# A decoder trunk in fp32 on one core: v's 512-column chunk goes first, and the first norm's gain moves behind the transposes

## The chip, the cores and the metric

The kernel runs on one core of one Trainium2 chip. The metric is the device time of one execution in microseconds (us). For the kernel before it is 1230.37, the median of three runs (1230.25 to 1230.64). One further execution was taken with the hardware profiler, and all rows of the trace come from it.

The engines are named as in the profile: PE (TensorE matmul), PEld (its weight loads), DVE (VectorE), ACT (ScalarE), POOL (GpSimd), SP (SyncE, which only issues DMAs here). L312 is line 312 of the kernel.

## The reference, cut to what matters

x has 512 tokens of 1024 features; there are two layers. The first mixes with a forgetting attention, the second with a gated short convolution; each is followed by a squared-ReLU MLP and a gated embedding. The change touches only the first norm and the first projections of the attention:

```python
def rmsnorm(x, g):
    y = x * lax.rsqrt(jnp.mean(x * x, axis=-1, keepdims=True) + RMS_EPS)
    return y * g

hn = rmsnorm(x, g[0])
proj = hn @ w_attn_in              # q, k, v: 1024 columns each; 16 forget-gate logits
v, f_logit = proj[..., 2*D:3*D], proj[..., 3*D:] + b_f
c = cumsum(log_sigmoid(f_logit))   # enters the scores as c_i - c_j
```

## The kernel before

**Numbers.** Everything is fp32. A factor is split in two fp32r parts, hi and lo (`split`, L270: ACT copies hi, then DVE or POOL subtracts it from the source for lo), and a product is three matmuls: hi*hi, lo*hi and hi*lo (`mm3`, L262).

**Layout.** The 512 tokens are four blocks of 128; a block's 1024 features are two pages of 128 x 512. `hT` holds the normed tokens turned, features on partitions, as a hi and a lo tile of eight 128-feature slices. A turned half block fills one bank of PSUM with four 128x128 transposes (`turned`, L309), and `keep` (L315) splits the whole bank into `hT`: one 128x512 copy on ACT, one 128x512 subtraction on DVE.

**The first norm.** `stats` (L298) squares both halves of a block on ACT (L295) with their sums, and `rstd` (L284) adds them and raises to the power -0.5 on POOL (L287, L290). `scaled` (L301) multiplies x by the inverse root and by the gain in one DVE operation (L303). The gain must stand in all 128 partitions: two 2 KB rows are loaded by POOL's DMAs and spread by PE's matmuls on a row of ones (L970 to L983) into two PSUM banks, which L303 reads.

**v.** `values(c, t)` (L438) makes one chunk c of v's columns for block t: eight features' slices, three matmuls each. `V_CHUNKS` gives the chunks and their order: first the last 256 columns of v together with the 16 logits (272 columns), then 512, then 256 columns. The function that it returns, `keep_v`, adds b_f to the logits (L454) and splits v into the pages `vs` by 128x128 copies and subtractions. So 96 matmuls stand behind each chunk: 4 blocks x 8 slices x 3.

**Weights.** `plan` lists all weights in order of use; `fetch` (L151) loads them on SP into 14 raw buffers, and `prepare` (L174) splits them into pages wh and wl, some eight ahead of use.

**What orders the work.** Within `manual_schedule` the order of the named engines is the one in the program's text; elsewhere a scheduler sets it. The opening is by hand on PE, DVE and ACT (L619 to L633): the norm of block 0, the first weights, then the four blocks through the 272-column chunk, each block's transposes in the middle (ahead of slice 5) of the block before. The loads of x and of the first eight weights are by hand on SP and ACT (L975 to L980), with b_f's load ahead of them on SP by the scheduler.

**After the opening.** `logs` (L397) makes log sigmoids of all logits, `sums_of_logs` (L419) their running sums by eight matmuls on a triangle (`tri`, L643) into `ps_c`; the sums go to DRAM and come back spread over partitions by `bias` (L498), with a select on POOL (L511). Then `project` (L470) makes q and k of two heads at a time (tile qk, 512 columns), and the scores (L516) begin. The first qk matmul is the first matmul behind v.

## Time and profile before

| | |
|---|---|
| median of three runs | 1230.37 us |
| the profiled execution | 1230.79 us |
| its span in the trace | 1229.1 us |
| mean granted PE clock | 0.997 |
| ACT busy | 676.4 us (55%) |
| POOL busy | 657.1 us (53%) |
| DMA, mean over the span | 121 GB/s |

The span runs from the first to the last instruction that the trace shows; a time in a row is counted from its start. A timeline row gives the start, the time from there to the end of the last of its instructions, the engine, line and operation, output<-inputs, shapes and count, and in brackets the idle time of the engine before it with what ended it. Matmuls are pipelined: the time of one in a row is longer than the distance of two starts. A row of a group gives after the count the busy time and the mean of one in ns, then the engine's idle time before them. A row of PE's waits gives us in total, times, and the longest. A row of windows gives the length, then the busy time of PE, PEld, DVE, ACT and POOL with their instructions, the granted PE clock, the share of the DMA engines and GB/s.

### The profile page before, as it was taken

The page shows a single profiled execution, that of the slowest core. Times are in us where ns is not written, and L with a number is a line of the kernel's source. Part 1 is how long each engine was busy: PE and PEld are TensorE (multiplying, and loading weights), DVE is VectorE, ACT ScalarE, POOL GpSimd, SP SyncE. Part 2 cuts the span into 40 slices and gives each one's busy share as a digit, 9 for nine tenths or more (in the row PEclk, how much of TensorE's full clock was granted, in tenths as well). Part 3 has the DMA queues.
Part 4 walks back from the last instruction along what each step waited for, and adds up shares of the span by engine and source line. Part 5 has one row for each costly group of instructions (what it writes and reads, how often), then busy time and mean ns, then how long its engine had stood idle before and what let it go on. Part 6 is the DMA issues. An engine that isn't in the chain of part 4 may idle for free.

```text
span 1229.1 us, 18662 instructions
## 1 busy us (share of the span) xinstructions
PE 1210.3 (98%) x6188; PEld 1030.5 (84%) x6188; DVE 912.2 (74%) x1410; ACT 676.4 (55%) x1429; POOL 657.1 (53%) x619
## 2 busy tenths in 40 slices
PE   7999999999999999999999999999999999999997
PEld 6888888898888888888889999989888888888886
DVE  5648878676778767869877798867776787669873
ACT  5447777556744654455565544445756345645551
POOL 2016656244977787775213255316677878678210
PEclk9999999999999999999999999999999999999999
DMA  7456564542343324428133033552422443236401
GB/s 251 149 157 172 143 172 113 167 149 78 103 137 105 98 73 137 132 68 296 57 100 108 30 104 95 156 174 74 137 78 60 137 138 99 64 113 180 162 18 52
DMA packets 85793, 148.73 MB, mean 121 GB/s; under 512 B 10112, under 2 KB 17328, under 8 KB 85696
## 3 DMA queue, kind: packets, MB, share of 16 engines
q1 hardware_dynamic: 85488, 147.27, 39.2%
q8 instruction: 49, 0.80, 0.3%
q14 instruction: 48, 0.39, 0.1%
q10 hardware_dynamic: 144, 0.26, 0.1%
q0 software_dynamic: 64, 0.00, 0.0%
HBM read 136.93 MB, written 6.37 MB: 117 GB/s over the span
## 4 chain that ended last, share of the span: by engine, by line
PE 96%; ACT 1%; DVE 1%; DMA 1%; issue 1%; POOL 1%; SPq 0%; DVEq 0%; POOLq 0%; ACTq 0%
PE up L266 9%; PE up L265 9%; PE up L264 9%; PE dn L264 8%; PE dn L265 8%; PE dn L266 8%; PE qk L265 2%; PE qk L264 2%; PE qk L266 2%; PE pg L265 2%; PE pg L264 2%; PE pg L266 2%; PE n_p L312 1%; PE pT L539 1%; PE v L264 1%; PE v L265 1%
## 5 line engine op out<-in xcount | busy, mean ns | idle before, releaser
L273 DVE TENSOR_TENSOR wl<-raw,wh 128x512 fp32r<-128x512 f32 (+1 forms) x398 | 377.3, 991 | 22.3 <-ACT wh L272 21.3
L272 ACT CAST wh<-raw 128x512 fp32r<-128x512 f32 (+1 forms) x398 | 217.5, 620 | 4.6 <-DVE xd L348 4.4
L265 PE MATMUL up<-hTh,wl 128*128 128x512 f32 (+1 forms) x576 | 210.2, 365 | 0.0
L266 PE MATMUL up<-hTl,wh 128*128 128x512 f32 (+1 forms) x576 | 209.7, 366 | 0.0
L264 PE MATMUL up<-hTh,wh 128*128 128x512 f32 (+1 forms) x576 | 208.7, 366 | 0.0
L820 ACT ACTIVATE r<-up 128x512 f32<-128x512 f32 (+1 forms) x72 | 39.4, 547 | 203.2 <-PE up L266 201.0
L273 POOL TENSOR_TENSOR wl<-dn_T,wh 128x512 fp32r<-128x512 f32 x96 | 132.6, 1413 | 30.1 <-ACT wh L272 30.1
L167 POOL TENSOR_TENSOR dn_T<-raw,raw 128x512 f32<-128x512 f32 x56 | 86.9, 1563 | 68.8 <-DMA raw<-in_wdn 58.3
L265 PEld LDWEIGHTS up<-hTh,wl 128*128 128x128 f32 x576 | 108.6, 189 | 17.5
L264 PEld LDWEIGHTS up<-hTh,wh 128*128 128x128 f32 x576 | 108.6, 189 | 17.6
L266 PEld LDWEIGHTS up<-hTl,wh 128*128 128x128 f32 x576 | 108.3, 189 | 17.5
L866 DVE TENSOR_TENSOR acc<-dn,acc 128x512 f32<-128x512 f32 x168 | 107.3, 679 | 14.9 <-PE dn L266 14.8
L167 POOL TENSOR_TENSOR dn_T<-raw,dn_T 128x512 f32<-128x512 f32 x56 | 92.4, 1650 | 2.2
L272 ACT CAST wh<-dn_T 128x512 fp32r<-128x512 f32 x112 | 61.4, 616 | 11.1 <-POOL dn_T L167 11.1
L273 DVE TENSOR_TENSOR A12l<-q,A12h 128x512 fp32r<-128x512 f32 x28 | 22.4, 801 | 55.0 <-ACT A12h L272 54.9
L880 POOL TENSOR_TENSOR acc<-acc,acc 128x512 f32<-128x512 f32 x28 | 46.9, 1706 | 9.9 <-DVE acc L866 9.9
L265 PE MATMUL qk<-hTh,wl 128*128 128x512 f32 x128 | 51.0, 399 | 0.0
L266 PE MATMUL qk<-hTl,wh 128*128 128x512 f32 x128 | 51.0, 398 | 0.0
L264 PE MATMUL qk<-hTh,wh 128*128 128x512 f32 x128 | 50.9, 398 | 0.0
L265 PE MATMUL pg<-wh,hTl 128*128 128x512 f32 x128 | 50.5, 394 | 0.0
L264 PE MATMUL pg<-wh,hTh 128*128 128x512 f32 x128 | 50.4, 394 | 0.0
L273 DVE TENSOR_TENSOR A11l<-q,A11h 128x256 fp32r<-128x256 f32 x28 | 23.1, 825 | 36.5 <-ACT A11h L272 36.5
(371 smaller groups left out, 3244.4 us busy)
## 6 DMA issues: line engine op xcount, KB each, us to landing
raw<-in_wup SPq DMA_DIRECT2D x128, 256.0 KB, 2.9
raw<-in_wdn SPq DMA_DIRECT2D x128, 256.0 KB, 2.8
raw<-in_wcq SPq DMA_DIRECT2D x36, 256.0 KB, 2.8
raw<-in_wqk SPq DMA_DIRECT2D x32, 256.0 KB, 3.4
raw<-in_wpg SPq DMA_DIRECT2D x32, 256.0 KB, 4.3
g<-in_g SPq DMA_DIRECT2D x22, 256.0 KB, 5.3
prl<-neg_c SPq DMA_DIRECT2D x16, 256.0 KB, 6.7
raw<-in_wo SPq DMA_DIRECT2D x16, 256.0 KB, 5.9
```

Source lines behind the costliest of these rows:

```text
L167: ins = nc.gpsimd.tensor_tensor(out=B[name], in0=B[a], in1=B[b], op=op)
L264: nc.tensor.matmul(ps, a.hi, b.hi, start=start, stop=False)
L265: nc.tensor.matmul(ps, a.lo, b.hi, start=False, stop=False)
L266: nc.tensor.matmul(ps, a.hi, b.lo, start=False, stop=stop)
L272: nc.scalar.copy(hi, src)
L273: return eng.tensor_tensor(out=lo, in0=src, in1=hi.bitcast(F32), op=ALU.subtract)
L312: nc.tensor.transpose(ps[:, j * P : (j + 1) * P], h[:, j * P : (j + 1) * P], ident)
L539: nc.tensor.transpose(ps[:, b * P : (b + 1) * P], probs[h][b][:, j * P : (j + 1) * P], ident)
L820: nc.scalar.activation(r[:, :n], ps[:, :n], AF.Relu)
L866: ins = nc.vector.tensor_tensor(out=a, in0=banks[s], in1=a, op=ALU.add)
L880: nc.gpsimd.tensor_tensor(out=a, in0=a, in1=acc[i, s][:, :S], op=ALU.add)
```

## The change

Five things change, all in the opening.

- **Order of the chunks.** The 512-column chunk comes first, then 272, then 256. The logits thus come with the second chunk: `logs` stands behind it, `sums_of_logs` behind block 2 of the third.
- **Two blocks through half the weights at a time.** The order is written out by hand on PE, DVE, ACT and now POOL: block 0 through weights 0 to 3, block 1 through them, block 0 through 4 to 7, then block 1; then blocks 2 and 3 as `values` does them. A block's hi*hi and lo*hi products of several slices go ahead of their hi*lo products. The lo parts of weights 0, 1, 2, 4, 5 and 6 are subtracted on POOL, those of 3 and 7 on DVE, each at a place of its own. The transposes of block 2 stand behind block 0's last product, those of block 3 behind block 1's.
- **The norm.** One half is squared on ACT, the other on DVE with its sum; DVE adds, POOL takes the power; DVE scales x by the inverse root without the gain.
- **The gain** is loaded as a column per slice (`g_col`, 128 x 8, on SP behind the first half block of x). `keep_rows` takes the place of `keep`: for each 128x128 piece of a bank ACT copies it times the gain to hT's hi, and DVE multiplies again and subtracts hi for lo. The gain's rows, PE's matmuls on ones that spread them, and their banks go.
- **Matmuls on ones.** `work(12)` issues twelve 128x512 matmuls on a page of ones, into a bank that nothing reads, ahead of the first transposes.

b_f is loaded behind x. The scheduler still orders the rest.

```diff
@@ -29,7 +30,7 @@
 PAGES = 70
 RAWS = 14
 LEAD = 1
-V_CHUNKS = ((768, 272), (0, 512), (512, 256))
+V_CHUNKS = ((0, 512), (768, 272), (512, 256))
 SOON = 8
 O_SOON = 1
 FEW = 4
@@ -66,7 +67,7 @@
 
 
 @with_exitstack
-def trunk(ctx: ExitStack, tc, x, pT, g, wv, wqk, bf, wo, wci, wcq, cw, wco, wup, wdn, wpp, wpg, out):
+def trunk(ctx: ExitStack, tc, x, pT, g, gT, wv, wqk, bf, wo, wci, wcq, cw, wco, wup, wdn, wpp, wpg, out):
     nc = tc.nc
     pool = lambda name, bufs, **k: ctx.enter_context(tc.tile_pool(name=name, bufs=bufs, **k))
     consts = pool("consts", 1)
@@ -171,7 +172,11 @@
                     mybir.DependencyInfo(mybir.DependencyClass.Sync, mybir.DependencyReason.DATA),
                 )
 
-    def prepare(upto):
+    def low_part(lo, src, hi, eng):
+        return eng.tensor_tensor(out=lo, in0=src, in1=hi.bitcast(F32), op=ALU.subtract)
+
+    def prepare(upto, held=None):
+
         while begun[0] < min(upto, len(order)):
             n = begun[0]
             begun[0] += 1
@@ -187,7 +192,11 @@
                 fetch(at + 1)
                 raw, eng, w = fetched[at], nc.vector, loads[at].shape[-1]
                 fetched[at] = None
-            split(hi[:, :w], lo[:, :w], raw[:, :w], eng)
+            if held is None:
+                split(hi[:, :w], lo[:, :w], raw[:, :w], eng)
+            else:
+                nc.scalar.copy(hi[:, :w], raw[:, :w])
+                held.append(partial(low_part, lo[:, :w], raw[:, :w], hi[:, :w]))
             ready[key] = Pair(hi[:, :w], lo[:, :w])
 
     def wide(*key, soon=SOON):
@@ -295,6 +304,14 @@
         nc.scalar.activation(junk, src, AF.Square, scale=D**-0.5, accum_out=ss)
         return ss
 
+    def products(src, name):
+        ss = stat(name)
+        nc.vector.tensor_tensor_reduce(
+            out=page(f"{name}_sq")[:, :S], in0=src, in1=src, scale=1.0 / D, scalar=EPS,
+            op0=ALU.mult, op1=ALU.add, accum_out=ss,
+        )
+        return ss
+
     def stats(t, xs, name):
         return rstd([squares(xs[n][:, :S], f"{name}_q{n}_{t}") for n in range(2)], f"{name}_r{t}")
 
@@ -385,9 +402,7 @@
                          f"{kind}r")
                 then(t)
 
-    def attention(hT, first_x, g0, by_hand):
-        b_f = consts.tile([P, H], F32, tag="bf", name="b_f")
-
+    def attention(hT, first_x, g_col, by_hand):
         vs = [[page(f"v{t}_{i}", F32R) for i in range(4)] for t in range(NB)]
         n_f = NB * H
         logit = stat("logit", n_f)
@@ -435,18 +450,17 @@
                 )
                 nc.sync.dma_start(neg_c[b, :, :n], t[:H, :n])
 
-        def values(c, t, soon=SOON, between=None):
+        def values(c, t, ps=None):
 
             c0, width = V_CHUNKS[c]
             n_v = min(width, D - c0)
-            ps = bank(f"v{c}_{t}")
-            for k in range(KT):
+            done = ps is not None
+            ps = ps if done else bank(f"v{c}_{t}")
+            for k in () if done else range(KT):
                 if width == 256:
                     w = wide("v", c, k // 2).at(lambda u: u[:, k % 2 * 256 : k % 2 * 256 + 256])
                 else:
-                    w = wide("v", c, k, soon=soon)
-                if k == 5 and between:
-                    between()
+                    w = wide("v", c, k)
                 mm3(ps[:, :width], tokens(hT, k, t), w, k == 0, k == KT - 1)
 
             def keep_v():
@@ -601,38 +615,111 @@
             prepare(where["o", 1, KT - 1] + 1)
             yield from out_part((0, 1), (6,))
 
-        nc.sync.dma_start(b_f, bf[0:1, :].partition_broadcast(P))
-        name = "n0"
-        E, done_v = mybir.EngineType, []
-
-        def rows(t):
-            r = stats(t, first_x[t], name)
-            return [scaled(t, n, first_x[t], r, g0, name) for n in range(2)]
+        name, E = "n0", mybir.EngineType
+        turns, banks_v = {}, [bank(f"v0_{t}") for t in range(2)]
+
+        def mean_squares(t):
+            half = lambda n: first_x[t][n][:, :S]
+            return squares(half(0), f"{name}_q0_{t}"), products(half(1), f"{name}_q1_{t}")
+
+        def inverse(t, q):
+            v, r = stat(f"{name}_v{t}"), stat(f"{name}_r{t}")
+            nc.vector.tensor_tensor(out=v, in0=q[0], in1=q[1], op=ALU.add)
+            nc.gpsimd.tensor_tensor(out=r, in0=v, in1=neg_half, op=ALU.pow)
+            return r
+
+        def scale_rows(t, r):
+            hs = []
+            for n in range(2):
+                hs.append(page(f"{name}_h{t}_{n}"))
+                nc.vector.tensor_scalar(
+                    out=hs[n][:, :S], in0=first_x[t][n][:, :S], scalar1=r, scalar2=None,
+                    op0=ALU.mult,
+                )
+            return hs
 
         def turn_rows(t, hs):
             for n in range(2):
-                keep(t, n, turned(t, n, hs[n], name), hT)
-
-        with tc.manual_schedule(engines={E.PE, E.DVE, E.Activation}):
-            r = stats(0, first_x[0], name)
-            prepare(3)
-            hs = {0: [scaled(0, n, first_x[0], r, g0, name) for n in range(2)]}
-            prepare(4)
+                turns[t, n] = turned(t, n, hs[n], name)
+
+        def keep_rows(t, n):
+            ps = turns.pop((t, n))
+            for j in range(4):
+                k = 4 * n + j
+                src, h = ps[:, j * P : (j + 1) * P], tokens(hT, k, t)
+                nc.scalar.mul(h.hi, src, g_col[:, k : k + 1])
+                nc.vector.scalar_tensor_tensor(
+                    out=h.lo, in0=src, scalar=g_col[:, k : k + 1], in1=h.hi.bitcast(F32),
+                    op0=ALU.mult, op1=ALU.subtract,
+                )
+
+        def part(t, k, p, of, start=False, stop=False):
+            nc.tensor.matmul(
+                banks_v[t], getattr(tokens(hT, k, t), p), getattr(ready["v", 0, k], of),
+                start=start, stop=stop,
+            )
+
+        def parts(t, ks, order, stop=False):
+            for p, of in order:
+                for k in ks:
+                    part(t, k, p, of, k == 0 and p == of, stop and k == ks[-1] and of == "lo")
+
+        HH, LH, HL = ("hi", "hi"), ("lo", "hi"), ("hi", "lo")
+        held = []
+
+        def low(eng):
+            held.pop(0)(eng)
+
+        with tc.manual_schedule(engines={E.PE, E.DVE, E.Activation, E.Pool}):
+            work(12)
+            r = inverse(0, mean_squares(0))
+            hs = scale_rows(0, r)
+            prepare(3, held)
+            low(nc.gpsimd)
+            low(nc.gpsimd)
+            turn_rows(0, hs)
+            keep_rows(0, 0)
+            prepare(4, held)
+            r = inverse(1, mean_squares(1))
+            parts(0, range(3), (HH, LH))
+            parts(0, range(3, 4), (HH, LH))
+            parts(0, range(2), (HL,))
+            last = held.pop()
+            last(nc.vector)
+            hs = scale_rows(1, r)
+            low(nc.gpsimd)
+            turn_rows(1, hs)
+            keep_rows(1, 0)
+            keep_rows(0, 1)
+            prepare(KT, held)
+            parts(1, range(4), (HH, LH))
+            parts(0, range(2, 4), (HL,))
+            parts(1, range(4), (HL,))
+            low(nc.gpsimd)
+            low(nc.gpsimd)
+            r = inverse(2, mean_squares(2))
+            hs = scale_rows(2, r)
+            low(nc.gpsimd)
+            keep_rows(1, 1)
+            low(nc.vector)
+            parts(0, range(4, KT), (HH, LH, HL), True)
+            turn_rows(2, hs)
+            r = inverse(3, mean_squares(3))
+            hs = scale_rows(3, r)
             for n in range(2):
-                keep(0, n, turned(0, n, hs[0][n], name), hT)
-                prepare(5 + n)
-            prepare(KT)
-            hs[1] = rows(1)
-            hs[2] = rows(2)
-            for t in range(NB):
-                between = (lambda: turn_rows(t + 1, hs[t + 1])) if t + 1 < NB else None
-                done_v.append(values(0, t, 0, between))
-                if t + 3 < NB:
-                    hs[t + 3] = rows(t + 3)
-                if t:
-                    prepare(KT + 3 * t)
-                    done_v.pop(0)()
-        done_v.pop(0)()
+                keep_rows(2, n)
+            values(0, 0, banks_v[0])()
+            parts(1, range(4, KT), (HH, LH, HL), True)
+            turn_rows(3, hs)
+            for n in range(2):
+                keep_rows(3, n)
+            values(0, 1, banks_v[1])()
+            for t in (2, 3):
+                done = values(0, t)
+                prepare(KT + 4 * t - 4, held)
+                while held:
+                    low(nc.gpsimd if len(held) % 2 else nc.vector)
+                done()
         tri = page("tri", F32R)
         ones = page("ones")
         nc.gpsimd.memset(ones[:, :S], 1.0)
@@ -641,15 +728,15 @@
             pattern=[[1, S]], channel_multiplier=-1,
         )
         nc.vector.tensor_copy(tri[:, :S], ones[:, :S])
+        for t in range(NB):
+            values(1, t)()
         logs()
         for t in range(NB):
-            values(1, t)()
+            values(2, t)()
             if t == 2:
                 sums_of_logs(tri)
         bias(0)
         bias(1)
-        for t in range(NB):
-            values(2, t)()
         for _ in project(0):
             pass
         main = stream()
@@ -967,24 +1054,28 @@
                 then(t)
 
 
-    one = page("one")
-    nc.vector.memset(one[:1, :P], 1.0)
-    rows = [page(f"row{n}") for n in range(2)]
-    for n in range(2):
-        nc.gpsimd.dma_start(rows[n][:1, :], g[0:1, n * S : (n + 1) * S])
+    warm = page("warm", F32R)
+    nc.vector.memset(warm[:, :S].bitcast(F32), 1.0)
+    g_col = consts.tile([P, KT], F32, tag="g_col", name="g_col")
     with tc.manual_schedule(engines={mybir.EngineType.SP, mybir.EngineType.Activation}):
         first_x = [load_x("xa", 0)]
+        nc.sync.dma_start(g_col, gT)
         fetch(4)
         first_x.append(load_x("xc", 1))
         fetch(KT)
         first_x += [load_x("xc", t) for t in (2, 3)]
-    g0 = [bank(f"g0_{n}") for n in range(2)]
-    for n in range(2):
-        nc.tensor.matmul(g0[n], one[:1, :P], rows[n][:1, :], start=True, stop=True)
+        b_f = consts.tile([P, H], F32, tag="bf", name="b_f")
+        nc.sync.dma_start(b_f, bf[0:1, :].partition_broadcast(P))
+
+    def work(n):
+        ps = bank("warm_p")
+        for _ in range(n):
+            nc.tensor.matmul(ps, warm[:, :P], warm[:, :S], start=True, stop=True)
+
     kept = dram.tile([2, NB, 2, P, S], F32, tag="kept", name="kept")
     hT = turned_x
     by_hand = ExitStack()
-    lhs, opened = attention(hT, first_x, g0, by_hand)
+    lhs, opened = attention(hT, first_x, g_col, by_hand)
     oT = lhs
     lhs = lambda k, t: tokens(oT, k, t)
     kind = "o"
@@ -1060,6 +1151,7 @@
 
     wa = np.asarray(w_attn_in)[0]
     got = {"x": np.asarray(x)[0], "g": np.asarray(norm_g).reshape(12, D)}
+    got["gT"] = got["g"][0].reshape(KT, P).T
     got["pT"] = np.asarray(p)[:, 0].reshape(2, S, 2, P).transpose(0, 3, 2, 1)
     for c, (c0, w) in enumerate(V_CHUNKS):
         got[f"wv{c}"] = tiles(wa[:, 2 * D + c0 : 2 * D + c0 + w], 2 if w == 256 else 1, w)[0]
```

1 line of the change is left out of this document (added).

## The prediction

> **What bounds the kernel now.** First the page: span, busy shares, the slices, the chain that ended last.
>
> ```profile
> span 1229.1 us, 18662 instructions
> ...
> PE 1210.3 (98%) x6188; PEld 1030.5 (84%) x6188; DVE 912.2 (74%) x1410; ACT 676.4 (55%) x1429; POOL 657.1 (53%) x619
> ...
> PE   7999999999999999999999999999999999999997
> ...
> PE 96%; ACT 1%; DVE 1%; DMA 1%; issue 1%; POOL 1%; SPq 0%; DVEq 0%; POOLq 0%; ACTq 0%
> ```
>
> PE is busy 98% of the span, in every slice but the first and the last, and 96% of the chain is PE. So the change, which touches only the opening, can move the end only by the time at which PE gets through that opening. I read PE's waits next, then PE's timeline.
>
> ```profile
> PE g L983 <- DMA row<-in_g: 6.4, 1, 6.4
> PE n_p L312 <- DVE n_h L303: 1.8, 1, 1.8
> 10.04 2.03 PE L312 MATMUL n_p<-ident,n_h 128*128 128x128 f32 x8
> 16.91 1.84 PE L312 MATMUL n_p<-ident,n_h 128*128 128x128 f32 x8 [1.84 <-DVE n_h L303]
> 19.00 0.43 PE L266 MATMUL v<-wl,hTh 128*128 128x272 f32 x1
> 19.23 0.43 PE L264 MATMUL v<-wh,hTh 128*128 128x272 f32 x1
> 21.06 0.29 PE L265 MATMUL v<-wh,hTl 128*128 128x272 f32 x1
> 21.19 0.29 PE L266 MATMUL v<-wl,hTh 128*128 128x272 f32 x1
> 22.44 1.03 PE L312 MATMUL n_p<-ident,n_h 128*128 128x128 f32 x8
> 23.23 0.37 PE L264 MATMUL v<-wh,hTh 128*128 128x272 f32 x1
> 36.22 0.39 PE L264 MATMUL v<-wh,hTh 128*128 128x512 f32 x1
> 36.45 0.39 PE L265 MATMUL v<-wh,hTl 128*128 128x512 f32 x1
> 47.78 0.40 PE L423 MATMUL ps_c<-tri,lf_h 128*16 128x512 f32 x1
> 48.95 0.44 PE L264 MATMUL v<-wh,hTh 128*128 128x512 f32 x1
> 54.48 0.28 PE L264 MATMUL v<-wh,hTh 128*128 128x256 f32 x1
> 65.99 0.40 PE L264 MATMUL qk<-hTh,wh 128*128 128x512 f32 x1
> ```
>
> The first column is the start. PE stands 6.4 us until the gain's rows land, spreads the gain, turns block 0 at 10.04, stands 1.8 us for block 1, and issues the first qk matmul at **65.99**. Start to start at full clock, a transpose takes 0.10 ((23.23 - 22.44)/8), a v matmul 0.125 at 272 columns, 0.227 at 512 ((47.78 - 36.22)/51, the count of such starts), and 0.12 at 256 ((65.99 - 54.48)/96); the sums of logs take 1.17 (47.78 to 48.95). Before 20.5 a 272-column matmul took 0.23: half clock.
>
> The scheduled order shows what follows the first qk matmul: the same PE sequence in both kernels, but for some ten swaps of neighbours. So the whole effect is the **shift of that matmul**. It is preceded by the same work in both: 32 transposes (3.2) + 96 x 0.227 (21.8) + 96 x 0.125 (12.0) + 96 x 0.12 (11.5) + 1.2 = **49.7 us**. Before: 10.04 + 49.7 = 59.7, so 6.2 is lost on the way, 1.8 of it in the one wait and most of the rest to the half clock.
>
> **The change part by part.** For each: its price, then where it lies.
>
> ```profile
> xa<-in_x ACTq DMA_DIRECT2D x1, 256.0 KB, 4.2
> 5.67 0.63 ACT L295 ACTIVATE junk<-xa 128x512 f32<-128x512 f32 x1 [3.15 <-DMA xa<-in_x]
> 6.42 0.63 ACT L295 ACTIVATE junk<-xa 128x512 f32<-128x512 f32 x1
> L290 POOL TENSOR_TENSOR n_r_y<-n_r_v,neg_half 128x1 f32<-128x1 f32 x4 | 2.4, 604 | 0.3
> L643 DVE CAST tri<-ones 128x512 fp32r<-128x512 f32 x1 | 0.4, 420 | 0.0
> L526 DVE CUSTOM_DVE_ANT_0 prl<-sc,prl 128x512 f32<-128x512 f32 x16 | 11.0, 687 | 4.4 <-PE pT L539 2.6 <-PE sc L524 1.1 <-DMA raw<-in_wo 0.7
> L303 DVE SCALAR_TENSOR_TENSOR n_h<-xd,n_r_y,g 128x512 f32<-128x512 f32 x24 | 17.0, 750 | 16.6 <-POOL n_r_y L290 16.6
> ```
>
> *Removed, a gain:* the two gain matmuls and their wait. b_f no longer stands ahead of x on SP, so that half lands as ACT's half does, near 0.8 + 4.2 = 5.0, not at 5.67 (bounds 4.7 and 5.6; the gain column and bigger first weights now share the DMA engines). The squares run side by side: ACT 0.75 (5.67 to 6.42), DVE's reduction 0.77 (0.69 by L526, the nearest form, and an estimated 0.08 for its sum): 5.8. An add (0.2, estimate) and POOL's power (0.60): 6.7. The row scale without gain has no row: between the one-operand cast at L643 (0.42) and the two-operand L303 (0.75). I take 0.42, as it too reads one page. **First transposes at 7.1**, 2.9 earlier. The 12 ones matmuls take 12 x 0.45 at half clock (an estimate by columns from 0.23 at 272) = 5.4, from about 1.4 (DVE's memset stands ahead of them), and lie wholly in PE's idle time; they can only help the clock.
>
> *Added, the main cost:* the gain moves into the copies behind the transposes. A bank was one 128x512 copy and one subtraction; it is now four 128x128 copies on ACT and four subtractions on DVE, and in the scheduled order ACT's copies 2 to 4 each wait for DVE's subtraction before. The nearest rows are the v evictions, with the same alternation:
>
> ```profile
> 26.90 0.27 ACT L272 CAST v<-v 128x128 fp32r<-128x128 f32 x1 [1.20 <-DVE logit L454]
> 27.20 0.29 DVE L273 TENSOR_TENSOR v<-v,v 128x128 fp32r<-128x128 f32 x1 [0.33 <-ACT v L272]
> 27.52 0.27 ACT L272 CAST v<-v 128x128 fp32r<-128x128 f32 x1 [0.36 <-DVE v L273]
> L749 ACT ACTIVATE za<-z,taps 128x512 f32<-128x512 f32 x6 | 4.3, 723 | 0.0
> L272 ACT CAST wh<-raw 128x512 fp32r<-128x512 f32 x390 | 214.6, 624 | 4.6 <-DVE xd L348 4.4
> L273 DVE TENSOR_TENSOR hTl<-n_p,hTh 128x512 fp32r<-128x512 f32 x40 | 26.3, 682 | 4.9 <-ACT hTh L272 4.9
> ```
>
> One pair takes 0.62 (26.90 to 27.52). A per-partition operand adds 0.10 on ACT (723 against 624) and 0.07 on DVE (750 against 682), 0.79 in all; by these rows, which have four times the columns, I take **0.77 a pair**, with bounds 0.79 and 0.62 (operands free). A bank therefore holds DVE for 3 x 0.77 + 0.29 = 2.6 us, where before DVE gave it 0.68 and ACT 0.59. Queued behind these pairs on ACT and DVE are the casts of the next weights, the next squares and, for wl3 and wl7, the subtractions; PE waits for them in turn.
>
> *Moved:* low parts of six first weights go to POOL, two stay on DVE.
>
> ```profile
> L273 DVE TENSOR_TENSOR wl<-raw,wh 128x512 fp32r<-128x512 f32 x24 | 15.6, 693 | 1.5 <-ACT wh L272 1.5
> L273 DVE TENSOR_TENSOR wl<-raw,wh 128x512 fp32r<-128x512 f32 x390 | 374.2, 1002 | 15.9 <-ACT wh L272 14.9
> L273 POOL TENSOR_TENSOR wl<-dn_T,wh 128x512 fp32r<-128x512 f32 x96 | 132.6, 1413 | 30.1 <-ACT wh L272 30.1
> 24.03 1.67 ACT L272 CAST wh<-raw 128x512 fp32r<-128x512 f32 x3
> ```
>
> DVE's subtraction takes 0.69 in the opening, where POOL has none, and 1.0 over the whole kernel, where POOL subtracts beside it; POOL's takes 1.41 then, and I take 1.35. A cast back to back takes 0.54 (1.67 less the tail, over 3).
>
> *The chain to block 2, us from the span's start.* Bank (0,0): four transposes to 7.7, 0.36 + 2.6, DVE done at 10.7, ACT at 10.3. wh3 and the square of block 1: 11.7; add, power, scale: transposes of block 1 at 12.9. Banks (1,0) and (0,1): ACT from 13.5, free at 18.8 (0.36 + 2 x 2.6, less 0.35 that is DVE's). wh4 to wh7: 20.9; POOL starts wl4 behind wh4, at 19.4, and ends wl5 at 22.1. Square of block 2: 21.7; its power stands behind wl5 on POOL: 22.7. Scale 0.84, with POOL's wl6 beside it, which I price at +0.4: 23.9. Bank (1,1): 26.5. wl7: 27.2. Only then does block 0's last product run, and behind it the transposes of block 2, at **27.4**. Then PE has done 16 transposes and 36 products at 512 columns, 9.8 us of work in 20.3: **10.5 idle**.
>
> *From 27.4:* PE has 16 transposes and 60 products ahead, 15.2, to 42.6. ACT and DVE have the rows of block 3 (to 29.5), four banks at 2.6 and two v evictions (3 x 0.62 + 0.29 = 2.1), 14.6 together, to 44.1, and the first 272-column cast stands behind them in the order: PE waits about **1.4**. The sums of logs come right behind the third block of v's last chunk. In the scheduled order their second operand, lf_l, stands on DVE behind three evictions, the first of which needs that very block: a copy of 0.27 and three or four steps of some 0.23 (estimated from the 0.29 row; starts are closer than ends) keep PE about **1.0**.
>
> *Sum:* 7.1 + 49.7 + 10.5 + 1.4 + 1.0 = 69.7, against 65.99: **+3.8 us**. The sooner start (2.9) and the 6.2 no longer lost are 9.1; the new waits cost 12.9.
>
> *The clock.*
>
> ```profile
> 17.10:20.50 3.40, 3.40 (x17) 3.33 (x17) 3.02 (x5) 2.27 (x5) 0.47 (x1) 0.50 1.06 379
> ```
>
> The column behind POOL is the granted clock: after the wait that ended at 16.91 one stretch of 3.4 us was granted 0.50. In the changed opening PE's waits between 22.6 and 27.2 are longer, so one such stretch at least is likely. It would cost up to 1.7 us (half of 3.4), but most falls where PE waits for DVE anyway, and the 1.4 before wh8 absorbs the rest: I add **+0.4**. The Trainium skill ("TensorE: Matmul & The Clock Gate", HAM oscillation — how this bites in real kernels) says that a wait longer than a window of about 3.4 us drops the clock to half, and its Part 4 says that transposes do not count as busy. The trace agrees on the half and the 3.4, though its wait was but 1.8. By that rule alone the term would be +1.7 and the time 1235.8.
>
> *Priced at nothing.* Logs, bias and scores:
>
> ```profile
> 65.90 0.29 POOL L511 TENSOR_SCALAR_AFFINE_SELECT prl<-prl 128x128 f32<-128x128 f32 x1 [0.63 <-DMA prl<-neg_c]
> 85.22 0.63 POOL L532 TENSOR_SCALAR prr<-prr,rs 128x128 f32<-128x128 f32 x1 [19.02 <-DVE rs L531]
> ```
>
> From the end of the sums (48.95) to the last select (66.2) it takes 17.2. They now end 24 x 0.12 = 2.9 before the first qk matmul, so the selects end 14.4 behind it; the first score is added on DVE just ahead of POOL's 85.22, some 17 behind it. 2.4 us of cover; if it went, only the excess would count. tri and ones have no reader before the sums. b_f is first read some 40 us after it is issued.
>
> So 1230.79 + 3.8 + 0.4 = 1235.0 in the profiled execution (span 1229.1 and 1.7 around it). The median of the runs shown, 1230.37, is 0.4 below that execution: **1234.5**.
>
> **The rivals.**
>
> *The opening works as drawn (other side: not slower).* The place is the alternation of ACT and DVE; its price is the pair. Ahead of 27.4 four banks stand on the path, 3 pairs of each: 12 us for 1 us on the pair. With free operands (0.62) 27.4 comes 1.8 sooner and the 1.4 before the 272-column products goes: 3.8 - 3.2 = +0.6, and the clock's term, which has then no cover, up to 1.7: 1231.0 to 1232.7. From a pair of **0.57** downward the first qk matmul is sooner than before. If a contiguous 128x128 copy is 0.16 cheaper than v's strided one (0.46: -1.9), x lands at 4.7 (-0.3), and the scale and POOL's subtractions are undisturbed (-0.8), it is -2.4, **1228.0**. For: every price is from a near row, not its own. Against: L749 and L303 both show the operand's surcharge.
>
> *The clock falls more often.* Two stretches at half clock, one in PE's own 15.2 us: +1.7 over my 0.4, so +5.9, 1236.3. For: the row of 17.10. Against: the cover named.
>
> *The row scale is dear or blocked.* At 0.75 each in three blocks on the path, +1.0; held up by POOL's whole wl6 (1.35 less my 0.4), +1.0 again: +6.2, 1236.6. With x at 5.6 (+0.6) and POOL's subtractions and power at 1.5 and 0.73 (+0.7) besides, +7.5, 1237.9. The Trainium skill ("SBUF — State Buffer", Who interferes with whom) says that DVE's two-port forms, a scale by one operand among them, and POOL lock each other out for a whole instruction; no row here shows such a scale beside POOL.
>
> *The ones matmuls do not raise the clock.* Block 0's products are then at half clock, but wait for pairs anyway: +0.5, inside the forecast.
>
> **How the numbers follow.** Forecast (+2.5 to +5.3) 0.45; as drawn 0.33, of which 0.12 is faster by over 0.2%, the rest about the +0.6 to +2.3; clock 0.11; scale 0.11. The range reaches from near that -2.4 to everything dear: 1228.0 to 1238.0, with some 0.15 outside. A measurement of this kernel can tell about 0.2%, 2.46 us. Slower by more: 0.45 less 0.04 at its lower edge, and 0.22: 0.63. Within: 0.25. Faster: 0.12.
>
> **What would show it.** Transposes of block 0 at 7.1, block 1 at 12.9, block 2 at 27.4; pairs of hTh and hTl 0.77 apart; the first 272-column product at 44; the first qk matmul at 70.2. It is wrong if ACT's copies run without waiting for DVE, if the pairs stay at 0.62 or less, if PE shows waits behind the first qk matmul that were not there, or if block 2 is turned before 25.

## The result, and the profile after

The changed kernel takes **1245.50 us** (median of four runs, 1245.17 to 1246.77) against 1230.31 for the kernel before: a ratio of 1.0126, 95% interval 1.0109 to 1.0144, or 15.2 us more. The forecast was 1234.5, its range 1228.0 to 1238.0. The direction was right; the size is 3.7 times that of the forecast and lies outside the range.

The page of the kernel after, in the order in which the page before was read:

```profile
span 1243.5 us, 18719 instructions
...
PE 1218.0 (98%) x6196; PEld 1034.7 (83%) x6196; DVE 922.2 (74%) x1440; ACT 679.8 (55%) x1445; POOL 662.9 (53%) x619
...
PE   6989999999999999999999999999999999999997
...
PE 91%; DVE 2%; issue 2%; ACT 1%; POOL 1%; DMA 1%; SPq 1%; POOLq 0%; DVEq 0%; ACTq 0%
```

The span is 14.4 us longer. PE still fills all slices but the first, the third and the last, but its share of the chain fell from 96% to 91%: more of the chain now runs through other engines and DMA. PE's waits (us in total, times, longest) say where:

```profile
PE n_p L329 <- DVE n_h L635: 3.7, 3, 2.1
PE sc L537 <- DMA kh<-kh: 3.6, 1, 3.6
PE v L657 <- DVE wl L176: 3.4, 1, 3.4
...
PE ps_c L438 <- DVE v L282: 0.9, 1, 0.9
PE sc L538 <- DMA kl<-kl: 0.9, 1, 0.9
```

The row left out is the 1.5 us ahead of the matmuls on ones, at the very start. Two of the five shown belong to the scores, not to the opening. PE's timeline splits the 14.4 in two:

```profile
7.84 0.66 PE L329 MATMUL n_p<-ident,n_h 128*128 128x128 f32 x4 [0.85 <-DVE n_h L635]
9.25 0.66 PE L329 MATMUL n_p<-ident,n_h 128*128 128x128 f32 x4 [0.75 <-DVE n_h L635]
15.34 1.09 PE L329 MATMUL n_p<-ident,n_h 128*128 128x128 f32 x8 [2.15 <-DVE n_h L635]
30.59 0.50 PE L657 MATMUL v<-wl,hTh 128*128 128x512 f32 x1 [3.39 <-DVE wl L176]
30.93 1.66 PE L329 MATMUL n_p<-ident,n_h 128*128 128x128 f32 x8
48.28 0.39 PE L273 MATMUL v<-wh,hTh 128*128 128x272 f32 x1 [0.17 <-ACT wh L281]
74.31 0.39 PE L273 MATMUL qk<-hTh,wh 128*128 128x512 f32 x1
94.37 0.64 PE L537 MATMUL sc<-kh,qs 128*128 128x128 f32 x3 [3.56 <-DMA kh<-kh]
95.90 1.01 PE L538 MATMUL sc<-kl,qs 128*128 128x128 f32 x3 [0.89 <-DMA kl<-kl]
```

The first qk matmul starts at 74.31 where it started at 65.99: **8.3 us are lost in the opening**. From there to the end of the span it took 1163.1 before (1229.1 - 65.99) and takes 1169.2 now (1243.5 - 74.31): **6.1 us are lost behind it**, at the first scores, which the prediction had priced at nothing. Such waits behind the first qk matmul, which were not there before, are one of the signs that the prediction itself had named for being wrong.

In the opening, DVE and POOL side by side:

```profile
6.30 2.89 DVE L635 TENSOR_SCALAR n_h<-xa,n_r 128x512 f32<-128x512 f32 x2 [0.75 <-POOL n_r L628]
13.80 1.87 DVE L635 TENSOR_SCALAR n_h<-xc,n_r 128x512 f32<-128x512 f32 x2 [0.45 <-POOL n_r L628]
25.41 1.90 DVE L635 TENSOR_SCALAR n_h<-xc,n_r 128x512 f32<-128x512 f32 x2 [0.66 <-POOL n_r L628]
32.08 1.46 DVE L635 TENSOR_SCALAR n_h<-xc,n_r 128x512 f32<-128x512 f32 x2 [0.67 <-POOL n_r L628]
```

```profile
6.23 2.68 POOL L176 TENSOR_TENSOR wl<-raw,wh 128x512 fp32r<-128x512 f32 x2
13.74 1.26 POOL L176 TENSOR_TENSOR wl<-raw,wh 128x512 fp32r<-128x512 f32 x1
25.34 1.29 POOL L176 TENSOR_TENSOR wl<-raw,wh 128x512 fp32r<-128x512 f32 x1
```

Each DVE row is the pair of row scales of one block, forecast at 0.84 a pair. The first three begin within 0.1 us of a POOL subtraction of a first weight and are 1 to 2 us longer than forecast; the fourth, beside no subtraction but POOL's filling of the page for the triangle, is 0.6 longer. The pairs behind the transposes, on the other hand, are as forecast: 0.79 from start to start.

```profile
16.81 0.37 ACT L650 ACTIVATE hTh<-n_p,g_col 128x128 fp32r<-128x128 f32 x1 [0.42 <-DVE hTl L651]
17.60 0.37 ACT L650 ACTIVATE hTh<-n_p,g_col 128x128 fp32r<-128x128 f32 x1 [0.42 <-DVE hTl L651]
```

At the scores, SP's issues (start, time of the issues, count) before, then after:

```profile
56.51 0.76 SPq L510 DMA_DIRECT2D prl<-neg_c  x1
58.08 12.10 SPq L157 DMA_DIRECT2D raw<-in_wqk  x8
72.26 0.53 SPq L495 DMA_DIRECT2D kh<-kh  x1
```

```profile
80.84 0.77 SPq L524 DMA_DIRECT2D prl<-neg_c  x1
81.70 4.98 SPq L158 DMA_DIRECT2D raw<-in_wqk  x3
86.77 0.53 SPq L509 DMA_DIRECT2D kh<-kh  x1
88.12 0.63 SPq L509 DMA_DIRECT2D kl<-kl  x1
```

The rows on neg_c are the bias rows of the first two heads, eight loads of 1.3 MB together; kh and kl are copied to their second half of the partitions by SP as well. Before, the last bias row was issued at 56.5, nearly sixteen us ahead of the first such copy. Now it is issued at 80.8, when kh is already made (80.6), the three weight loads that follow take 5 us to issue, and the copies go out from 86.8 on, 6.2 us behind kh. The view of DMA issues from 60 to 98 us (KB each, median us to landing; before, then after) shows that they then also land late:

```profile
kh<-kh SPq DMA_DIRECT2D x4, 128.0 KB, 3.2
kl<-kl SPq DMA_DIRECT2D x4, 128.0 KB, 2.9
```

```profile
kh<-kh SPq DMA_DIRECT2D x4, 128.0 KB, 7.1
kl<-kl SPq DMA_DIRECT2D x3, 128.0 KB, 7.0
```

So PE stood 3.6 and 0.9 us for kh and kl, and paid once more behind the wait; in the windows the granted clock is the third figure from the end:

```profile
96.00:97.00 1.00, 1.00 (x4) 1.00 (x5) 0.59 (x3) 0.25 (x1) 0.00 (x0) 0.52 0.98 209
97.00:98.00 1.00, 1.00 (x4) 0.71 (x4) 0.90 (x5) 0.87 (x4) 0.47 (x1) 0.50 0.91 289
```

Half clock from 96.0 to 99.4 (its end by windows of 0.2 us) costs 1.6 to 1.7. 3.6 + 0.9 + 1.6 = 6.1. By the rule of the clock's page in the Trainium skill ("TensorE: Matmul & The Clock Gate", HAM oscillation — how this bites in real kernels) a wait of that length is paid for twice; here the trace agrees, with 0.50 behind 3.6 us.

### The profile page after: what moved, and what is told of

The parts are those of the page before. It is cut to its first block, busy times and chain, and to the rows that moved or that the text cites. A ratio compares the mean times of both kernels' runs of the same rounds, so it can differ in the third digit from the quotient of the medians.

```text
span 1243.5 us, 18719 instructions
## 1 busy us (share of the span) xinstructions
PE 1218.0 (98%) x6196; PEld 1034.7 (83%) x6196; DVE 922.2 (74%) x1440; ACT 679.8 (55%) x1445; POOL 662.9 (53%) x619
## 4 chain that ended last, share of the span: by engine, by line
PE 91%; DVE 2%; issue 2%; ACT 1%; POOL 1%; DMA 1%; SPq 1%; POOLq 0%; DVEq 0%; ACTq 0%
PE up L275 9%; PE up L274 9%; PE up L273 9%; PE dn L273 8%; PE dn L275 8%; PE dn L274 8%; PE pg L273 2%; PE pg L275 2%; PE pg L274 2%; PE qk L274 2%; PE qk L273 2%; PE qk L275 2%; PE pT L553 1%; PE o L273 1%; PE o L275 1%
## 5 line engine op out<-in xcount | busy, mean ns | idle before, releaser
L281 ACT CAST wh<-raw 128x512 fp32r<-128x512 f32 (+1 forms) x390 | 212.9, 620 | 4.6 <-DVE xd L365 4.4
L273 PEld LDWEIGHTS up<-hTh,wh 128*128 128x128 f32 x576 | 108.6, 189 | 17.5
L275 PEld LDWEIGHTS up<-hTl,wh 128*128 128x128 f32 x576 | 108.3, 189 | 17.4
L275 PE MATMUL pg<-wl,hTh 128*128 128x512 f32 x128 | 50.2, 392 | 0.0
```

What stands on the lines that cost most here:

```text
L273: nc.tensor.matmul(ps, a.hi, b.hi, start=start, stop=False)
L275: nc.tensor.matmul(ps, a.hi, b.lo, start=False, stop=stop)
L281: nc.scalar.copy(hi, src)
```

## The experiments

The theory formed from these rows: (1) the pairs cost what was forecast, (2) the row scales are held up by POOL's subtractions, (3) the sums of logs, which now end just ahead of the first qk matmul instead of 17 us ahead of it, put the bias rows ahead of the copies of kh and kl. Rivals: the scale is slow by itself; the pairs carry all of the opening; the wait at the scores only follows from the late opening; SP's order alone, not the load on the DMA engines, makes it.

Each kernel's first qk matmul comes from the view of the tile qk, "rest" is its span less that start. Kernels a, b, c, d, e, i, l and o ran once, so a difference of 1 or 2 us can be one of executions (the seven of m2 span 2.6); the other times are medians. First qk and rest are those of the execution with the trace. "before" is the kernel before beside it.

| kernel | time | before | first qk | rest |
|---|---|---|---|---|
| before | 1230.31 | | 66.0 | 1163.1 |
| after | 1245.50 | 1230.31 | 74.3 | 1169.2 |
| a: POOL's subtractions on DVE | 1242.45 | 1230.71 | 71.4 | 1169.3 |
| b: kh, kl on ACT's queue | 1245.33 | 1230.71 | 74.4 | 1169.2 |
| c: whole-bank copies | 1236.39 | 1230.71 | 65.0 | 1169.7 |
| d: no matmuls on ones | 1247.74 | 1229.68 | 75.1 | 1170.9 |
| e: before, order of the chunks alone | 1235.83 | 1230.71 | 64.2 | 1169.9 |
| i: bias rows free of the sums | 1238.62 | 1229.68 | 74.1 | 1162.8 |
| l: a, c and i together | 1224.89 | 1229.68 | 60.7 | 1162.5 |
| k: before, with ones in its waits | 1228.87 | 1229.68 | 64.7 | 1162.4 |
| m2: a, c, gain back in the norm | 1233.62 | 1229.77 | 63.4 | 1168.5 |
| m: m2, head 1's bias rows later | 1227.97 | 1229.77 | 63.4 | 1163.4 |
| n: after, head 1's bias rows later | 1240.41 | 1229.68 | 75.1 | 1165.8 |
| o: row scale on two pages | 1248.95 | 1229.68 | 75.8 | 1171.4 |

The last column has two levels, about 1163 and 1168.5 to 1171.4, with n between them. Every kernel that keeps the late sums with all their bias rows is on the upper one, whatever its opening does.

What makes the upper level is PE's waits for kh and kl and the clock behind them. In windows of 0.2 us the stretch at half clock behind the first qk matmul is 3.4 us long in the kernel after and in m2, 6.8 in a, b, c, d, e and o, and absent in the others. Less those waits and half of that stretch, the last column is 1162 to 1163.5 for every kernel but n.

**a. POOL's subtractions on DVE.**

```diff
-            low(nc.gpsimd)        # six places
+            low(nc.vector)
```

> The changed kernel with the six POOL subtractions of the first weights moved to DVE, each at its own place in the order; nothing else. Theory (the row scales are held up by POOL's subtractions): with no POOL subtraction in the opening each of the eight 128x512 scales takes 0.40 to 0.45 us, where the changed kernel's pairs of scales took 2.89, 1.87, 1.90 and 1.46; DVE pays 6 x 0.69 for the subtractions, so the first qk matmul comes only 0 to 2 us sooner than 74.3. Rival (a scale by one operand is slow by itself): the pairs of scales still take 1.5 or more, and the first qk matmul comes at 76 or later.

The views of the tile n_h (least, median and greatest ns) of the kernel after and of this one:

```profile
L635 DVE TENSOR_SCALAR n_h<-xa,n_r x2: 1485/1486/1486, 6.3 to 7.7; 128x512 f32<-128x512 f32 x2
```

```profile
L635 DVE TENSOR_SCALAR n_h<-xa,n_r x2: 481/484/486, 6.4 to 6.8; 128x512 f32<-128x512 f32 x2
```

A scale takes 0.48 without POOL beside it and 1.49 with it: the theory holds (0.48 is a little above its 0.40 to 0.45), the rival of a scale that is slow by itself falls. Only block 3's pair, beside POOL's filling of the page for the triangle, still takes 1.46. The first qk matmul came 2.9 sooner, more than the 0 to 2 expected, although DVE took over six subtractions.

**c. Whole-bank copies.** The first norm's gain is left out.

```diff
-            for j in range(4):
...
-                nc.scalar.mul(h.hi, src, g_col[:, k : k + 1])
-                nc.vector.scalar_tensor_tensor(...)
+            keep(t, n, ps, hT)
```

> The changed kernel with each turned bank split by one 128x512 copy on ACT and one 128x512 subtraction on DVE, as before; this leaves the first norm's gain out. Theory (the 128x128 pairs, 0.79 us each, take about 3.5 us off the opening between block 0 and block 2, and the scales held by POOL take as much): the first qk matmul comes 3 to 5 us sooner, at 69.3 to 71.3, still later than 65.99. Rival (the pairs carry nearly all): it comes 7 to 8 us sooner, at 66 to 67. Rival (they are hidden): within 1 us of 74.3.

The first qk matmul is at 65.0, 9.3 sooner: the rival that the pairs carry nearly all of the opening's loss comes closest, and the expectation of 3 to 5 was too small. It had forgotten the prediction's own price: 1.9 us a bank (2.6 against 0.68), for the four banks ahead of block 2, are 7.7. Block 2's transposes start at 23.22 instead of 30.93, just that. The other 1.6 lie behind them, 0.9 of it the wait at the sums, which is gone. The scales beside POOL are as long here as in the kernel after.

**e. The order of the chunks alone, in the kernel before.**

```diff
-V_CHUNKS = ((768, 272), (0, 512), (512, 256))
+V_CHUNKS = ((0, 512), (768, 272), (512, 256))
...
-        logs()
         for t in range(NB):
             values(1, t)()
-            if t == 2:
-                sums_of_logs(tri)
-        bias(0)
-        bias(1)
+        logs()
         for t in range(NB):
             values(2, t)()
+            if t == 2:
+                sums_of_logs(tri)
+        bias(0)
+        bias(1)
```

> The kernel before with the order of v's chunks alone changed (512, 272, 256), logs behind the 272-column chunk and the sums behind block 2 of the last; norm, gain, copies and the order by hand stay. Theory (the later sums press bias rows and weights ahead of the copies of kh and kl): the first qk matmul moves by less than 2 us, and the first scores wait 3 to 5 us for kh or kl; 3 to 7 us slower than before. Rival (that wait comes from the whole opening being late): no such wait, within 2 us of before.

```profile
PE sc L523 <- DMA kh<-kh: 3.2, 1, 3.2
PE sc L524 <- DMA kl<-kl: 0.9, 1, 0.9
```

With the opening 1.8 us sooner than before, the waits for kh and kl are there all the same, and the kernel is 5.1 us slower than the one before. The rival that the wait follows from a late opening falls: the order of the chunks makes it, by where it puts the sums.

**b. kh and kl on ACT's queue.**

```diff
-                            nc.sync.dma_start(h[b, :S]..., h[a, :S]...)
+                            (nc.sync if i else nc.scalar).dma_start(h[b, :S]..., h[a, :S]...)
```

> The changed kernel with the four copies of kh and kl of the first two heads issued on ACT's DMA queue instead of SP's. The first score stood 3.6 and 0.9 us for them. Theory (they stand behind the bias rows and weight loads in SP's order): they are issued near 81 to 83 instead of 86.8 to 90.6, the two waits shrink to under 1 us together and the time falls by 3.5 to 6 us, to 1239.5 to 1242. Rival (the DMA engines are full of bias rows, whoever issues): issued sooner, they land as late, and the waits stay above 3 us.

```profile
PE sc L537 <- DMA kh<-kh: 2.7, 1, 2.7
PE sc L538 <- DMA kl<-kl: 0.6, 1, 0.6
```

```profile
84.58 0.52 ACTq L509 DMA_DIRECT2D kh<-kh  x1
87.75 0.47 ACTq L509 DMA_DIRECT2D kl<-kl  x1
88.26 0.58 ACT L281 CAST kh<-qk 64x512 fp32r<-64x512 f32 x1 [7.64 <-DMA pr<-neg_c]
```

The time is the same, and the rest too, against the theory; the rival's sign, waits above 3 us, is there. But not because nothing moved. ACT issued the first copies 2.2 and 0.4 us sooner than SP had, and the first scores of each follow 0.8 and 1.2 sooner (93.58 and 94.66 for 94.37 and 95.90), so the waits are 3.3 instead of 4.5. What this won the clock took: half clock lasts 6.8 us behind these waits, where it lasted 3.4 in the kernel after. A row of windows:

```profile
93.40:100.00 6.60, 5.79 (x16) 4.76 (x17) 5.60 (x16) 5.67 (x12) 1.90 (x3) 0.50 0.75 226
```

Nor was the issue moved far. ACT itself stood 7.6 us until a bias row landed (its copies wait for an earlier DMA in the scheduled order), so the first copy left 4.0 us behind kh (80.6), and it took 8.9 us to land where SP's took 7.5. So b does not settle whether SP's order or the load on the DMA engines makes the copies late; n, below, says more.

**i. Bias rows free of the sums.** The bias rows of heads 0 and 1 come from an input, which leaves their true bias out.

```diff
-                nc.sync.dma_start(pr, neg_c[b, h : h + 1, :n].partition_broadcast(P))
+                nc.sync.dma_start(pr, (neg_c[b, h : h + 1, :n] if h > 1 else g[h : h + 1, :n]).partition_broadcast(P))
...
+        bias(0)
+        bias(1)
         for t in range(NB):
             values(1, t)()
```

> The changed kernel with the bias rows of the first two heads read from an input (the norms' gains) ahead of v's second chunk, so that these eight loads no longer follow the sums of logs; this leaves the true bias out of heads 0 and 1. Theory (the late sums put 1.3 MB of bias rows and the weights behind them ahead of the copies of kh and kl, and the DMA engines are full): the first score's waits for kh and kl, 3.6 and 0.9, go below 0.5 together, the half clock behind them too, the first qk matmul stays within 1 us of 74.3 and the time falls by 5 to 6.5 us, to 1239 to 1240.5. Rival (the weights alone fill the engines): waits of 2 us or more stay.

The waits for kh and kl are gone from PE's list, the rest is 1162.8, and the time 1238.6, 6.9 less, a little more than the 5 to 6.5 expected. SP issues the first copy as soon as kh is made (80.34), and it lands 4.0 us later. This is (3) by itself, 6.4 us in that column.

**d. No matmuls on ones.**

```diff
-            work(12)
```

> The changed kernel without the twelve matmuls on ones. Theory (they bring the clock up before block 0, where PE waits for ACT's and DVE's pairs anyway): block 0's 512-column products take 0.43 to 0.45 instead of 0.23 from start to start, the first qk matmul comes 0 to 1 us later than 74.3, the time changes by less than 1.5 us. Rival (they carry the opening): the first qk matmul comes 2 us later or more.

The first qk matmul comes 0.8 later, within the theory. The whole is 2.2 us slower than the median after, more than expected. Its rest is 1.7 longer, and the traces have the place: the stretch at half clock behind the scores' waits is 6.8 us here (94.5 to 101.3), 3.4 in the kernel after. On one execution each, nothing shows that this hangs on the ones: a, b and c keep the ones, e never had them, and all four have 6.8 as well.

**l. All three undone.** The edits of a, c and i; the gain and the bias are left out.

> The changed kernel with three things undone at once: the first weights' subtractions on DVE instead of POOL, whole-bank copies behind the transposes (the first norm's gain left out), and bias rows of heads 0 and 1 from an input ahead of v's second chunk (their true bias left out). Theory (these three are all that makes the change slow): the first qk matmul at 63 to 65, no wait for kh, and 1227 to 1230, not slower than before. Rival (something else is slow as well, such as the order by halves or the norm on two engines): first qk matmul at 67 or later, or more than 1232.

1224.9, 4.8 us *faster* than the kernel before, and the first qk matmul 5.3 sooner, both better than the theory's 1227 to 1230 and 63 to 65. PE's timelines show how the costs add up:

| kernel | block 2's transposes | first 272-column product | first qk |
|---|---|---|---|
| after | 30.9 | 48.3 | 74.3 |
| a | 28.3 | 45.6 | 71.4 |
| c | 23.2 | 40.3 | 65.0 |
| l | 20.5 | 36.0 | 60.7 |

Ahead of block 2 they simply add: 2.7 by a, 7.7 by c, 10.4 by l. From there to the first 272-column product, 15.2 us of work for PE, l takes 15.4 and the other three 17.1 to 17.4. In each of those three a stretch of 3.4 us at half clock begins within 0.6 us of block 2's transposes, worth up to 1.7; l has none. That accounts for l's 13.6 in the first qk matmul, where a and c win only 12.2 together.

Part of the gain over the kernel before is what l leaves out; with the gain in place, m2 below, 2.6 are left in the opening. That much the rest of the change (512 columns first, two blocks through half the weights, the norm on two engines, the ones) is worth there, and the three costs hid it. What each of these parts is worth is not shown: the order of the chunks alone (e) wins 1.8 and ones alone (k) 1.3, and neither of the two, nor m2, has the stretch at half clock that the kernel before has right behind block 1's transposes (17.1 to 20.5).

**k. The kernel before with ones in its waits.**

```diff
+    work(10)                       # ahead of the gain's matmuls
...
+                    if t == 0:
+                        work(8)    # ahead of block 1's transposes
```

> The kernel before with ten matmuls on ones ahead of the gain's and eight in the wait ahead of block 1's transposes; nothing else. Theory (half clock after PE's waits costs the opening before some 4 us, and PE is what bounds the opening from block 1 on): the stretch from 17.1 to 20.5 is granted full clock, the first qk matmul comes 1 to 2 us sooner than 65.99 and the time is 1 to 2 us shorter, 1228.4 to 1229.4. Rival (the products of block 0 then end sooner and the wait for block 1 grows by the same, or the ones delay it): within 0.7 us of before.

1228.87 against 1229.68, ratio 0.9990 (0.9980 to 0.9999), the first qk matmul 1.3 sooner, as the theory had it; the time, 0.8 less, is a little under its 1 to 2, and the interval only just clears 1. The half clock has not gone, it lies earlier (8.2 to 15.0), and the products behind block 1's transposes are at full clock. Those transposes did not start sooner (16.85 for 16.91), although DVE began their scales 0.76 sooner (15.35 for 16.11): the eight matmuls on ones hold PE until then. Whether fewer would win more was not tried.

**m2 and m. The gain in place.** Whole-bank copies and DVE's subtractions, the gain again in the norm's scale (`g_col` now names the two banks that hold it), with its rows on ACT's queue and spread behind eight matmuls on ones; m also moves head 1's bias rows.

```diff
-            work(12)
+            work(8)
+            spread()               # two matmuls, a row of ones by the gain's rows
...
-                nc.vector.tensor_scalar(out=hs[n][:, :S], in0=..., scalar1=r, ...)
+                nc.vector.scalar_tensor_tensor(
+                    out=hs[n][:, :S], in0=..., scalar=r, in1=g_col[n][:, :S], op0=ALU.mult, op1=ALU.mult)
...
         bias(0)
-        bias(1)                    # m alone
         for _ in project(0):
             pass
+        bias(1)                    # m alone
```

> The changed kernel with two of its three dear things undone and the gain in place: the first weights' subtractions on DVE, whole-bank copies behind the transposes, and the gain back in the norm's scale (rows loaded on ACT's queue, spread by two matmuls on a row of ones behind eight of the matmuls on ones). The late sums of logs stay. Theory: as with all three undone, less the 0.3 us by which each of the scales is longer and the spreading: first qk matmul at 61 to 63.5; the late sums cost what they cost before, 6 to 8 us; 1231 to 1234, a little slower than before. Rival (the wait for kh is smaller when DVE and ACT are less pressed): 1227 to 1230.

> The same, and the bias rows of head 1 loaded behind the first projection instead of ahead of it, so that half of the bias rows no longer stands ahead of the copies of kh and kl. Theory (the DMA engines are filled by bias rows and the weights behind them): the wait of the first score falls from 3 to 5 us to 1 to 2, the clock stays up, and the time is 2 to 5 us less than without this edit, 1227 to 1230. Rival (head 1's scores then wait for its own rows, by as much): within 1 us of it.

```profile
PE sc L537 <- DMA kh<-kh: 2.8, 1, 2.8
PE sc L538 <- DMA kl<-kl: 1.2, 1, 1.2
```

```profile
PE sc L538 <- DMA kl<-kl: 0.2, 1, 0.2
```

m2 has its first qk matmul at 63.4, in the range expected, and the old wait: 1233.62, ratio 1.0028 (1.0017 to 1.0039). m, with half of the bias rows out of the way, has 0.2 us of it left, less than the 1 to 2 expected: **1227.97**, ratio 0.9984 (0.9974 to 0.9993). It is the version that beats both kernels, by 0.16% against the one before. That moving one call takes 5.6 us away is the plainest sign that the bias rows ahead of kh and kl were the cause.

**n. The same one edit in the changed kernel.**

```diff
         bias(0)
-        bias(1)
         for _ in project(0):
             pass
+        bias(1)
```

> The changed kernel with one edit: the bias rows of head 1 are loaded behind the first projection instead of ahead of it. Theory (the late sums cost some 6.6 us by the bias rows and weights ahead of the copies of kh and kl): the waits of the first scores fall from 4.5 to under 1, the first qk matmul stays at 74 to 74.6, and the time falls by 4.5 to 6.5 us to 1238.5 to 1241. Rival (in the changed kernel the sums end so much later against qk that half of the rows is too much as well): 1 to 3 us.

1240.41, 5.1 less than the median after (ratio to before 1.0086, 1.0069 to 1.0103), within the range expected. Of the waits 0.6 is left:

```profile
PE sc L538 <- DMA kl<-kl: 0.6, 1, 0.6
```

```profile
83.66 0.53 SPq L509 DMA_DIRECT2D kh<-kh  x1
```

kh is made at 81.4 here, so SP issues its copy 2.3 us behind it, where the kernel after took 6.2; the copy then takes 7.7 us to land, for 7.5. The waits fell by 3.9 and the delay of the issue by the same: this gain comes from SP's getting to the copies sooner, not from a faster copy. So the rival that SP's order makes the wait is right for this part, and the theory's filled DMA engines are seen only in the copies' 7 to 9 us. Why each weight load ahead of the copies takes 0.9 to 2.4 us to issue in the kernel after is not shown. The execution with the trace was the longest of four (1242.61; the others 1240.2 to 1240.5): its first qk matmul is at 75.1 for the 74 to 74.6 expected, and a transpose waited 1.3 for POOL's scaling of a probability row, so its rest is not the typical one.

**o. The row scale on two pages.**

```diff
-                nc.vector.tensor_scalar(out=..., in0=..., scalar1=r, scalar2=None, op0=ALU.mult)
+                nc.vector.scalar_tensor_tensor(out=..., in0=..., scalar=r, in1=warm[:, :S].bitcast(F32), op0=ALU.mult, op1=ALU.mult)
```

> The changed kernel with the row scale as an operation on two pages (times the inverse root, times a page of ones), POOL's subtractions beside it as they are. Theory (a scale of one page by one operand stands still until POOL's subtraction beside it is done): with two pages DVE and POOL share instead, each scale takes 0.75 alone and 1.0 to 1.4 beside POOL, so the pairs of scales take 2.0 to 2.6 where they took 2.89, 1.87 and 1.90, and block 3's, with no POOL subtraction beside it, takes 1.5. Rival (POOL slows any form alike, by stretching): the pairs take 3.5 or more in block 0.

```profile
L635 DVE SCALAR_TENSOR_TENSOR n_h<-xa,n_r,warm x2: 741/1240/1740, 6.4 to 8.0; 128x512 f32<-128x512 f32 x2
```

0.74 alone (the least) and 1.74 beside POOL (the greatest): the loss is 1.0 us, just as with one page (0.48 to 1.49). The first half of the theory, that two pages share better, falls: 1.74 is above its 1.0 to 1.4, although the pairs, 2.40 in the first three blocks, are in its 2.0 to 2.6. The rival's 3.5 did not show either. POOL's second subtraction began at 8.24, when the second scale had been running for 0.2 us; the scale kept its 0.74, and the subtraction took 1.67 for the 1.26 of the first. In both meetings the one that began later was the longer one. So a DVE operation of 128x512 loses 1.0 us to a POOL subtraction of 1.3 that began just before it, in either form. Whether DVE stands still or is stretched, these rows do not tell.

## Why the prediction was wrong, step by step

Between the forecast's first qk matmul, 70.2, and the measured 74.31 lie 4.1 us, 3.5 of them ahead of block 2's transposes (30.93 for 27.4); the 6.1 at the scores come on top.

- **What bounds the kernel: right as far as it went.** PE's way through the opening sets the end. "So the whole effect is the shift of that matmul" was wrong: the order of PE's instructions is the same behind it, but not what they wait for. The shift is 8.3 of the 14.4.
- **"Priced at nothing. Logs, bias and scores": the step that failed, 6.1 us.** It followed the bias rows to the selects and the scores, and found 2.4 us of cover. That chain does hold: no score waited for a select. What it left out are the other DMAs of the same stretch: the copies of kh and kl, which the first score needs as well, and which lie behind the bias rows. The row of SP that shows them nearly 16 us apart before was not used. i, e, n and m against m2 show it.
- **The row scales: mis-sized.** 0.42 each without a word on POOL in blocks 0 and 1, and 0.42 with 0.2 more in block 2. This is the step that failed in the opening. Without POOL it is 0.48; beside a POOL subtraction 1.49. Of the pairs forecast at 0.84, three took 2.89, 1.87 and 1.90, and block 2's transposes came at 30.93 instead of 27.4. By a, 2.7 us ahead of block 2 hang on it, and 2.9 in the first qk matmul. This was the rival "dear or blocked", at 0.11; its time, 1236.6, priced one such meeting at 1.35 where there were four. The rule of the Trainium skill ("SBUF — State Buffer", Who interferes with whom), that such a scale and POOL hold each other up, stood there for wl6 alone; the runs agree that DVE is held up, with 0.48 against 1.49, in every block where a POOL subtraction is near, though by 1.0, less than the 1.26 of the subtraction.
- **The pairs: right.** 0.79 measured for 0.77; and 7.7 us ahead of block 2 by c, as the prediction's price of a bank gives for four banks.
- **The start: 0.7 late, by two errors against each other.** x landed at 4.4 to 4.6, not 5.0, but the first scale took 1.49 for 0.42: 7.84 for 7.1.
- **The waits behind block 2 and the clock: the sum near, its parts not.** From the transposes of block 2 to the first 272-column product it took 17.4 for 16.6 to 16.7, and the wait at the sums was 0.9 for 1.0. But the wait of 1.4 ahead of that product was 0.2; in its place stands a stretch at half clock, 31.1 to 34.5, in PE's own work, as the rival "The clock falls more often" had it, at 0.11. The other stretch, 17.5 to 24.3, lies under DVE's chain, as the forecast said: PE still waited 3.4 for DVE behind it. The stretch behind the scores had no term, as there was no wait in the sum to lose it behind.
- **The sum itself** is 0.1 off: 69.7 less 65.99 is 3.7, not 3.8.
- **The rivals.** "As drawn" falls: it needed a cheaper pair than 0.77, and the pair was 0.79. That m is 1.8 us faster than the kernel before does not bear it out, since m leaves the pairs aside. The range was too narrow since its dear end held only the opening's prices.

## What to carry to other kernels

When a step moves to a later place, follow every DMA that it issues, and then list what stands behind them in the issuing queue and on the DMA engines in the stretch where they land; the transfer that was early and idle comes to stand ahead of one that is urgent. Take the price of a DVE operation from a row with the same neighbour on POOL, not from a row of its own. And an edit with three costs and one gain can look like a bad idea: undo the costs one at a time before dropping it.

## What the runs showed of the hardware that was not expected

- A 128x512 DVE scale loses 1.0 us to a POOL subtraction of 1.3 us that began just before it, with one page read (0.48 to 1.49) and with two (0.74 to 1.74) alike; a subtraction that began 0.2 us into a scale was itself the longer one (1.67 for 1.26).
- Behind eight broadcast bias rows and the weights, a copy of 128 KB took 7.5 us from issue to landing, where the same copy took 2.3 in the kernel before and 4.0 in i. On ACT's queue, issued 2.2 us earlier, it took 8.9 and landed 0.8 sooner (b).
- Every stretch at half clock in the first 120 us of the fourteen traces lasted 3.4 us or 6.8 us. A wait of 1.8 us in the kernel before and one of 3.6 at the scores were followed by 3.4, one of 2.7 in b by 6.8, so that a shorter wait did not mean less time lost.
